# Moving a short convolution from TensorE to ScalarE and VectorE in a scheduled decoder layer

## The chip, the cores and the metric

The kernel runs on the 8 cores of one Trainium2 chip; every core works on one sequence of the batch. The time is that of the slowest core, in microseconds (us), as the device reports it. Below, PE is TensorE, DVE is VectorE, ACT is ScalarE, POOL is GpSimd and SP is SyncE, as the profile calls them. Some executions fall into a slow state, in which the cores of one die, sometimes of both, get a lower clock (0.95 to 0.81 of full speed, where the others have 0.99); only fast executions are compared.

The time before was 769.93 us (median of 6, 769.37 to 770.86).

## The reference

One decoder layer on x of 2048 x 1024 per core: two sub-layers, each with a norm before and a norm after, both scaled by a conditioning vector.

```python
def token_mixer(h, ...):
    z = einsum("bsd,dk->bsk", h, w_in)
    gb, gc, v, a, g = split(z)
    y_short = gb * causal_dwconv(gc * v, w_short, b_short)   # 3 taps, 512 channels
    u = causal_dwconv(a * sigmoid(g), w_cfm_dw, b_cfm_dw)    # 31 taps
    y_cfm = silu(layernorm(u))
    y = per_head_rmsnorm(concat(y_short, y_cfm)) * beta
    return einsum("bsm,md->bsd", y, w_out)                   # "out-projection"

h = modulate(rmsnorm(x, g_pre), shift1, scale1)
x = x + gate1 * rmsnorm(token_mixer(h), g_post)
h = modulate(rmsnorm(x, g_pre_ffn), shift2, scale2)
x = x + gate2 * rmsnorm(swiglu_ffn(h), g_post_ffn)
```

## The kernel before

The kernel is written as a list of operations with a cost each. When it is built, a scheduler of its own lays them out in time and fixes the order in which every engine works. The program gives each engine its list in that order, with waits on semaphores.

```python
def schedule(self):
    ...
    for s_, issue in succ[i]:        # when may a successor of o start, in the scheduler's reckoning?
        r = free[e] if issue or (e == "pe" and s_.eng == "pe") else \
            o.done + (0.0 if s_.eng != "pe" else MARGIN if o.dma is None else LATE ...)
    ...
MARGIN = 200.0                       # slack (ns) before an instruction of TensorE
```

The short convolution: a projection into one PSUM bank, three taps as matmuls with diagonal weights into a second one, then the product.

```python
def short(q):                                        # q: one of 4 chunks of 512 positions
    ... for j in range(4):
        proj(b3, wb, j * 1024, q, "pb", also=[b4])   # 8 matmuls 128x512
        act(bs, b3.v(), AF.Identity, bias=..., name="b_ev")
        for d in range(3):
            mm(b4.v(), dg3.v(i*128, i*128+128), rv_, d == 0, d == 2, name="sconv")
        dve("scalar_tensor_tensor", ..., name="ysh", in0=b4.v(), in1=bs, ...)
        ...                                          # squares, head statistics, norm
```

The out-projection, one tile of 128 positions after the other. Between its tiles TensorE works on other matmuls (the projections "pb" of later chunks, gate and up of the feed-forward part), here called filler.

```python
def outproj(q, pairs):
    for b in range(4):
        xt = Tile(xc_s).v()
        dma("pool", [(xt, xq[q, b])], ..., 1.35, "xload2")      # residual, on GpSimd's queue
        ...                                                     # and weight loads, same queue
        pt = pair('op', *pairs)                                 # two PSUM banks
        for n_, k in enumerate(korder):
            for hf in range(2):
                mm(pt.v(hf*512, hf*512+512, part=hf), yT..., wo..., name="oproj")
        post(pt.v(), xt, 0, 16 + i, xb_.v())
        dma("sp", [(x1q[q, b], xt)], [xt], ..., 1.95, "x1st")   # store; its landing frees xt
        last = norm_cast(xt, 32 + i, xb_.v())                   # pre-norm of the feed-forward part

def post(pv, xt, l, i, junk):
    tv = Tile(pg_s[l]).v()                                      # one product buffer
    dve("tensor_tensor", [pv, gtg], [tv], 1225, "po_g")         # product with the gate
    act(junk, pv, AF.Square, n=1024, accum=sm(SM_SSQ + i), name="po_sq")
    rsqrt_col(i, "po_rs", ...)          # two [128,1] steps on GpSimd: add EPS, then power -0.5
    dve("scalar_tensor_tensor", [tv, ("rs", i), xt], [xt], 1290, "po_add")
```

## Time and profile before

| | before |
|---|---|
| time, median | 769.93 us |
| spans of the cores in the profiled run | 764.2 to 768.6 us |
| TensorE busy | 736.7 us (96%) |
| out-projection, first to last matmul (core 4) | 208.6 to 335.6 us |

The head of the profile's page, for the slowest core: the span, then busy time and instructions of each engine.

```profile
span 768.6 us, 11317 instructions; the slowest of 8 cores (764.2 to 768.6 us)
...
PE 736.7 (96%) x4191; PEld 370.7 (48%) x4191; DVE 303.7 (40%) x464; ACT 266.7 (35%) x460; POOL 133.7 (17%) x271
```

The windows view of core 4: bounds and length of a stretch, then busy time (and instructions) of PE, PEld, DVE, ACT and POOL, the granted clock, the DMA share and GB/s.

```profile
0.00:33.00 33.00, 12.20 (x121) 7.39 (x122) 10.67 (x51) 9.00 (x18) 16.99 (x37) 0.95 0.94 190
...
211.00:338.00 127.00, 126.63 (x658) 59.62 (x657) 76.44 (x91) 74.19 (x118) 41.07 (x88) 1.00 0.74 178
```

In the out-projection stretch TensorE is busy all the time and the other three look half idle: VectorE 60%, ScalarE 58%, GpSimd 32%. The waits view of TensorE for the same stretch (waiter, what ended the wait, us in total, times, longest) has one entry:

```profile
PE ps L760 <- DVE xn_98 L594: 0.4, 1, 0.4
```

What a tile of the out-projection needs from the other engines is a chain. The timeline of one tile of core 4 (start, duration, engine, line, operation, what it writes and reads):

```profile
291.63 1.22 DVE L594 TENSOR_TENSOR pga_126<-ps,gtg_123 128x1024 f32<-128x1024 f32 x1 [1.78 <-PE ps L578]
...
292.94 1.02 ACT L590 ACTIVATE xn_96<-ps 128x1024 bf16<-128x1024 f32 x1 [1.85 <-DVE pga_126 L594]
...
294.22 0.22 POOL L598 TENSOR_SCALAR small<-small 128x1 f32<-128x1 f32 x1 [2.02 <-ACT xn_96 L590]
...
294.59 0.57 POOL L598 TENSOR_TENSOR small<-small 128x1 f32<-128x1 f32 x1
...
295.33 1.28 DVE L594 SCALAR_TENSOR_TENSOR xc_83<-pga_126,small,xc_83 128x1024 f32<-128x1024 f32 x1 [1.82 <-POOL small L598]
```

Product, squares, two small steps on GpSimd, add: from 291.63 to 296.62, that is 4.99 us, and the next tile's product may not start before, since there is one product buffer. In this part the first matmuls of successive tiles start at 287.8, 294.3, 300.8 and 307.3 us: one tile in 6.5 us.

### The profile page before, as it was taken

How to read it: one execution, taken by the hardware profiler on the slowest of the kernel's cores; microseconds unless marked ns; L12 is line 12 of the kernel's file. 1: busy time of each engine (PE TensorE's matmuls, PEld its weight loads, DVE VectorE, ACT ScalarE, POOL GpSimd, SP SyncE). 2: the span in 40 equal slices, each digit the busy share in tenths (PEclk: the TensorE clock that was granted, in tenths of full speed). 3: DMA queues.
4: the chain of work that ended last, by engine and by line, in shares of the span. 5: the costliest groups of instructions: out<-in, count | busy, mean ns of one | idle time of the engine just before them, and what ended most of it. 6: DMA issues, size and time to landing. Idle time of an engine off the chain costs nothing.

```text
span 768.6 us, 11317 instructions; the slowest of 8 cores (764.2 to 768.6 us)
## 1 busy us (share of the span) xinstructions
PE 736.7 (96%) x4191; PEld 370.7 (48%) x4191; DVE 303.7 (40%) x464; ACT 266.7 (35%) x460; POOL 133.7 (17%) x271
## 2 busy tenths in 40 slices
PE   0899999999999999999999999999999999999996
PEld 0587568544444444544444444444444444444442
DVE  3343876956657665553221221222221212112222
ACT  1255558884566854543111111111111111111112
POOL 4543212412103153332010000000000000000000
PEclk9998999999999999999999999999999999999999
DMA  8999538998694768889986395333434433001321
GB/s 185 197 240 218 99 86 115 145 164 138 157 194 139 182 153 204 202 211 195 179 156 119 55 142 133 109 110 110 110 55 82 84 56 54 1 0 56 113 87 75
DMA packets 36806, 98.16 MB, mean 128 GB/s; under 512 B 4112, under 2 KB 12432, under 8 KB 33424
## 3 DMA queue, kind: packets, MB, share of 16 engines
q0 software_dynamic: 20048, 66.92, 48.0%
q1 hardware_dynamic: 16704, 30.52, 12.1%
q8 instruction: 34, 0.56, 0.3%
q14 instruction: 20, 0.16, 0.1%
HBM read 125.54 MB, written 16.78 MB: 185 GB/s over the span
## 4 chain that ended last, share of the span: by engine, by line
PE 92%; DMA 2%; POOL 2%; ACT 1%; issue 1%; DVE 1%; DVEq 0%; SPq 0%; POOLq 0%; ACTq 0%
PE ps L578 90%; DMA xa_75<-x 2%; PE ps L760 2%; POOL small L598 1%; ACT hT L590 0%; DVE xc_85 L594 0%; ACT xn_97 L590 0%; ACT xn_98 L590 0%; DVE xn_98 L594 0%; POOL wdn_65 L610 0%; DVE xc_84 L594 0%; DVEq L419 0%; DVE pga_126 L594 0%; ACT xn_96 L590 0%; POOL wdn_64 L610 0%
## 5 line engine op out<-in xcount | busy, mean ns | idle before, releaser
L578 PE MATMUL ps<-hT,slot_46 128*128 128x512 bf16 x512 | 113.9, 379 | 0.0
L578 PE MATMUL ps<-wdn_64,actT 128*128 128x512 bf16 x512 | 113.3, 379 | 0.0
L578 PE MATMUL ps<-hT,slot_43 128*128 128x512 bf16 x448 | 102.1, 379 | 0.0
L578 PE MATMUL ps<-hT,slot_45 128*128 128x512 bf16 x448 | 99.6, 379 | 0.0
L578 PE MATMUL ps<-hT,slot_44 128*128 128x512 bf16 x384 | 84.7, 379 | 0.0
L578 PEld LDWEIGHTS ps<-wdn_64,actT 128*128 128x128 bf16 x512 | 50.1, 98 | 60.4
L578 PEld LDWEIGHTS ps<-hT,slot_46 128*128 128x128 bf16 x512 | 50.1, 98 | 58.2
L578 PEld LDWEIGHTS ps<-hT,slot_43 128*128 128x128 bf16 x448 | 43.5, 98 | 51.7 <-issue 1.4
L578 PEld LDWEIGHTS ps<-hT,slot_45 128*128 128x128 bf16 x448 | 43.7, 98 | 50.6
L598 POOL TENSOR_SCALAR small<-small 128x1 f32<-128x1 f32 x62 | 15.9, 256 | 291.9 <-ACT xn_95 L590 136.4
L578 PEld LDWEIGHTS ps<-hT,slot_44 128*128 128x128 bf16 x384 | 37.4, 98 | 45.2
L594 DVE TENSOR_TENSOR pgb_127<-ps,gtg_124 128x1024 f32<-128x1024 f32 (+1 forms) x17 | 19.7, 1162 | 76.0 <-PE ps L578 75.9
L578 PE MATMUL ps<-wdn_65,actT 128*128 128x512 bf16 x192 | 44.2, 379 | 0.0
L598 POOL TENSOR_TENSOR small<-small 128x1 f32<-128x1 f32 x62 | 38.7, 624 | 8.6 <-POOL small L598 0.6
L594 DVE TENSOR_TENSOR actT<-ev_107,ps 128x512 bf16<-128x512 f32 x22 | 15.1, 686 | 52.6 <-PE ps L578 52.6
L594 DVE TENSOR_TENSOR actT<-ev_108,ps 128x512 bf16<-128x512 f32 x22 | 15.1, 686 | 50.3 <-PE ps L578 50.1
L594 DVE TENSOR_TENSOR actT<-ev_110,ps 128x512 bf16<-128x512 f32 x22 | 15.1, 686 | 50.1 <-PE ps L578 50.1
L594 DVE TENSOR_TENSOR actT<-ev_109,ps 128x512 bf16<-128x512 f32 x22 | 15.1, 686 | 48.6 <-PE ps L578 48.6
L590 ACT ACTIVATE ev_107<-ps 128x512 f32<-128x512 f32 x22 | 13.1, 597 | 54.4 <-PE ps L578 54.4
L590 ACT ACTIVATE ev_110<-ps 128x512 f32<-128x512 f32 x22 | 13.1, 597 | 53.2 <-PE ps L578 53.2
L590 ACT ACTIVATE ev_108<-ps 128x512 f32<-128x512 f32 x22 | 13.1, 596 | 51.7 <-PE ps L578 51.7
L578 PE MATMUL ps<-wo_63,yT 128*128 128x512 bf16 x128 | 30.9, 379 | 0.0
(328 smaller groups left out, 963.8 us busy)
## 6 DMA issues: line engine op xcount, KB each, us to landing
slot_46<-wgu POOLq DMA_DIRECT2D x6, 1024.0 KB, 11.9
slot_44<-wgu POOLq DMA_DIRECT2D x6, 1024.0 KB, 10.6
slot_45<-wgu POOLq DMA_DIRECT2D x5, 1024.0 KB, 16.0
slot_43<-wgu POOLq DMA_DIRECT2D x5, 1024.0 KB, 11.2
wdn_64<-wdn POOLq DMA_DIRECT2D x16, 256.0 KB, 13.4
slot_44<-wada POOLq DMA_DIRECT2D x12, 256.0 KB, 10.7
slot_43<-wada POOLq DMA_DIRECT2D x2, 1024.0 KB, 12.7
slot_45<-wada POOLq DMA_DIRECT2D x8, 256.0 KB, 15.0
```

What stands on the lines that cost most here:

```text
L578: return P.op("pe", lambda e: e.matmul(out.ap, lhsT=lhsT.ap, rhs=rhs.ap, start=start, stop=stop), reads=[lhsT, rhs] + list(reads), writes= ...
L590: return P.op("act", lambda e: e.activation(out=out.ap, in_=in_.ap, **a), reads=[in_] + list(reads), writes=[out] + list(writes), cost=c, ...
L594: return P.op("dve", lambda e: getattr(e, meth)(**{k: val(v) for k, v in kw.items()}), reads=reads, writes=writes, cost=cost, lat=80.0, na ...
L598: return P.op("pool", lambda e: getattr(e, meth)(*a, **kw), reads=reads, writes=writes, cost=cost, lat=80.0, name=name)
L760: P.op("pe", lambda e, ov=ov, iv=iv: e.transpose(out=ov.ap, in_=iv.ap, identity=ident.t[:, :]), reads=[iv, ident.v()], writes=[ov], cost=6 ...
```

## The change

Its intent is to take 52 short-conv matmuls from TensorE, to halve the norm of the out-projection so that VectorE and ScalarE read its two PSUM banks at the same time, to build the weights of the long convolution more cheaply, to load inputs in another order, and to give the scheduler costs and slack that fit the chip better. The core of the diff:

```diff
 def short(q):
-    b3, b4 = bank('sm', 0, 1, 2, 3), bank('sm', 0, 1, 2, 3)
-    proj(b3, wb, j * 1024, q, "pb", also=[b4])
-    act(bs, b3.v(), AF.Identity, ..., name="b_ev")
-    for d in range(3): ...
-        mm(b4.v(), dg3.v(...), rv_, d == 0, d == 2, name="sconv")
+    ac = accd[q, j] if q < 2 else taps(q, j)      # chunks 0 and 1 were done early
+    b3 = bank('sm', 0, 1, 2, 3)
+    proj(b3, wb, j * 1024, q, "pb")
+def taps(q, j):
+    act(dst, src, AF.Identity, scale=w, bias=vc(V_BSH + j), npt=2, name="sconv")       # tap 0
+    dve("scalar_tensor_tensor", [src, dst, K_V], [dst], 210 + 1.055 * n * PT, "sconv") # taps 1, 2
 ...
 def post(pv, xt, l, i, junk):
+    if l == 0:
+        for z in range(2):
+            for y, hv_ in ((z, "g"), (1 - z, "s")):      # one bank for VectorE, the other for ScalarE
+                ... dve("tensor_tensor", ..., 690, "po_g") / act(..., AF.Square, ..., name="po_sq")
+        pool("tensor_scalar", ..., 350, "po_rs", ..., op0=ALU.add, op1=ALU.add)
+        pool("tensor_tensor", ..., 640, "po_rs", ..., op=ALU.pow)
+        dve("scalar_tensor_tensor", ..., 1290, "po_add")
 ...
-    for half in range(2): warm(...); xload(0, (2, 3), "pool") ...
+    NAMES = ["x00", "a0.x01.a1.x10.g0.g1.x11.g2.g3.h0.x2.wv.h1.x3"]    # order of the first loads
 ...
-    c = 200 + 0.833 * n + 70 * npt + (190 if accum is not None else 0)
+    c = 95 + 0.833 * n + (0, 60, 180)[npt] + (80 if accum is not None else 0)
 ...
-RAW_SHIFT = 250.0
-MARGIN = 200.0
+RAW_SHIFT = 400
+MARGIN = 500
+PAD = 40
```

## The prediction

> **What bounds the kernel now.** TensorE: 96% busy on the page, 92% of the chain of waits. Start-to-start times prove it: in the timeline sixteen 128x512 matmuls take from 82.29 to 85.75 us, 0.216 us each, which agrees with N/2.4+2.5 ns in the Trainium skill, "TensorE: Matmul & The Clock Gate" (Back-to-back issue gap). From 80 us to the end TensorE keeps that spacing; the waits list has only some 1 us for it after 92 us (0.5 us at 285 us and 0.45 us at 349 us, transposes waiting for xn_98 of the out-projection). Its other lost time is in the first 80 us: 17.4 us until the second x tile lands (17.8 us) and is normalised, 1.8 us at 28.5 us, 1.3 us at 73.5 us, and stretches at half clock (starts 0.427 us apart from 75 to 80 us; granted clock 0.76 between 66 and 80 us in the windows view). DMA is saturated until about 75 us.
>
> **Removed.** The short convolution's matmuls: 44 of 512 columns and 8 of 256. 44 x 0.216 + 8 x 0.109 = 10.4 us, all between 195 and 257 us where TensorE never waits, so all on the critical path. Also the diagonal weights (12 x 0.18 us VectorE) and 16 b_ev evictions (0.69 us ScalarE).
>
> **Added.** 16 accumulators: one ScalarE pass (est. 0.7 us, as b_ev of the same size) and two VectorE passes of 0.75 us (as glu and ysh). VectorE +24 us, ScalarE about even. Half lands in 143 to 200 us; both engines are full (19.6 and 19.5 of 20) only between 140 and 160 us, and VectorE is half free afterwards, so it is absorbed. The rest lands in 200 to 257 us, where VectorE is 63% busy. The convolution weights built from a broadcast (16 x 1.48 us) get perhaps 10 us of VectorE cheaper, off the path.
>
> **Moved.** The halved norm reads the two PSUM halves by VectorE and ScalarE at once. Per tile po_g (1.22) and po_sq (1.02+0.19) ran one after the other; now 2 x 0.69 beside 2 x (0.6+0.19): about 1 us less in a loop that has one product buffer and turned every 6 us. It keeps out-projection fed with fewer filler matmuls, and removes most of the two holes. The load order moves the same bytes and does not shorten the first wait. It should spread the sparse one-column matmuls that precede the half-clock stretch at 72 to 80 us; I credit 2.3 us, uncertain. Weight loads have 16 us of slack or more from 190 to 430 us, so arriving 10 us earlier does not run into DMA.
>
> **Sum.** 769.9 - 10.4 - 2.3 (start) - 0.9 (out-projection) = 756.3 us, range 752.5 to 760.5. Faster by over 2% 0.30, within 2% 0.69, slower 0.01.
>
> **What would show it.** TensorE matmuls down by 52; no cvb matmuls; span after 100 us shorter by about 11 us; TensorE waits after 92 us under 2 us; cw builds near 0.8 us; po_g as 32 halves near 0.69 us; the first gate-weight matmuls still near 35 us, and the half-clock stretch near 75 us shorter or gone.
>
> **What would make it wrong.** VectorE falling behind between 140 and 260 us (TensorE gaps before the y statistics, out-projection or its transposes); gate weights landing 5 us later and starting dense work later, costing 3 to 5 us; or a start that gains more, losing both the half-clock stretch and the waits before 35 us.

## The result and the profile after

The time after was 768.84 us (median of 20, slow ones included), beside 770.41 us for the kernel before on the same chip. The fast runs alone have medians of 766.76 (12 runs) and 770.24 us (35 runs). The ratio is 0.9956, with a 95% interval of 0.9945 to 0.9967: the same within 2%, about 3.4 us less. All ratios here are the mean time of one kernel's fast runs over that of the other's in the same rounds; the medians quoted can include slow runs, so a ratio isn't quite that of the medians.

The head of the page after:

```profile
span 765.9 us, 11358 instructions; the slowest of 8 cores (758.8 to 765.9 us)
...
PE 729.8 (95%) x4139; PEld 365.9 (48%) x4139; DVE 316.0 (41%) x505; ACT 270.6 (35%) x492; POOL 136.4 (18%) x271
```

The 52 matmuls are gone, yet TensorE's share of the span fell. The following table gives medians over the eight cores of start times in us. The waits of TensorE are the distance between the starts of successive matmuls beyond what their size takes at full clock, summed. They are idle time. Of the time lost at half clock they hold only what smaller matmuls lose: a 512-column matmul at half clock starts its successor 0.21 us late, which looks like a matmul that is missing from the record, and such excesses are left out. With half clock counted, the medians of most runs rise by 0.4 us at most, but those of e1, e3 and e4 (below) to 8.5, 6.9 and 8.6 us.

| milestone | before | after | difference |
|---|---|---|---|
| first gate-weight matmul | 33.3 | 34.6 | +1.3 |
| first matmul of the long convolution | 105.5 | 104.8 | -0.7 |
| first out-projection matmul | 211.3 | 213.1 | +1.8 |
| last out-projection matmul | 338.3 | 331.2 | -7.1 |
| last matmul | 760.3 | 755.2 | -5.1 |
| span | 767.1 | 761.6 | -5.5 |
| waits between first and last out-projection matmul | 0.7 | 6.0 | +5.2 |

So 5.2 of the 10.4 us came back as waits in one stretch. (Which fillers fall before the first out-projection matmul differs between the two orders, so single rows don't add up.) The windows view of core 4 after, same columns:

```profile
0.00:35.00 35.00, 12.54 (x123) 7.07 (x123) 10.95 (x45) 11.46 (x22) 20.68 (x44) 0.95 0.94 194
...
212.00:332.00 120.00, 115.71 (x599) 53.65 (x600) 83.77 (x115) 71.39 (x142) 48.30 (x88) 1.00 0.80 189
```

TensorE idles 4.3 us of these 120 where it idled 0.4 of 127. VectorE is at 70% and GpSimd at 40%: not full on average. The waits view of TensorE for this stretch:

```profile
PE ps L583 <- DVE pga_133 L599: 2.2, 2, 2.0
PE ps L583 <- ACT xn_104 L595: 1.2, 1, 1.2
PE ps L583 <- issue: 0.6, 2, 0.4
PE ps L762 <- DVE xn_105 L599: 0.5, 1, 0.5
```

The first two are projection or out-projection matmuls that wait for a PSUM bank which VectorE (pga, the product) or ScalarE (xn, the squares) has not read yet; the last are transposes that wait for a pre-norm (xn_105).

The average of VectorE hides the longest wait. The windows view of core 4 around it, and lines of the timeline:

```profile
231.00:237.00 6.00, 3.97 (x18) 1.45 (x17) 5.58 (x8) 5.18 (x10) 2.30 (x5) 1.00 0.54 203
...
234.03 0.74 DVE L599 SCALAR_TENSOR_TENSOR yT<-ys_120,vt,rs_124 128x512 bf16<-128x512 f32 x1
...
234.70 0.68 DVE L599 TENSOR_TENSOR pga_133<-ps,gtg_130 128x512 f32<-128x512 f32 x1
...
235.30 0.74 DVE L599 SCALAR_TENSOR_TENSOR yT<-ys_121,vt,rs_124 128x512 bf16<-128x512 f32 x1
...
235.96 0.68 DVE L599 TENSOR_TENSOR pga_133<-ps,gtg_130 128x512 f32<-128x512 f32 x1
...
236.89 2.10 PE L583 MATMUL ps<-hT,slot_43 128*128 128x512 bf16 x9 [2.00 <-DVE pga_133 L599]
```

VectorE is busy 5.58 of these 6 us (5.5 on the other cores), and its order puts two passes of the short convolution's norm (yT) before and between the two halves of the product. Here VectorE does fall behind.

The groups view of core 4 shows the pieces: new accumulator passes, the halved product, and the two GpSimd steps in the out-projection stretch (busy us, mean ns of one, idle time before them and what ended it). First the GpSimd lines of the kernel before, from 208 to 337 us:

```profile
L598 POOL TENSOR_TENSOR small<-small 128x1 f32<-128x1 f32 x30 | 17.1, 571 | 4.0
L598 POOL TENSOR_SCALAR small<-small 128x1 f32<-128x1 f32 x30 | 7.9, 265 | 73.2 <-ACT xn_95 L590 33.7 <-ACT xn_96 L590 18.3 <-ACT xn_97 L590 14.0
```

The same view of the kernel after, GpSimd from 212 to 332 us and the other two engines from 100 to 340 us:

```profile
L603 POOL TENSOR_TENSOR small<-small 128x1 f32<-128x1 f32 x30 | 18.3, 610 | 4.4 <-POOL small L603 0.4
L603 POOL TENSOR_SCALAR small<-small 128x1 f32<-128x1 f32 x30 | 13.3, 443 | 64.2 <-ACT xn_102 L595 33.5 <-ACT xn_103 L595 12.2 <-ACT xn_104 L595 10.9
...
L599 DVE TENSOR_TENSOR pga_133<-ps,gtg_130 128x512 f32<-128x512 f32 x32 | 22.0, 689 | 12.7 <-PE ps L583 8.2 <-ACT xn_102 L595 1.3 <-DVE pga_133 L599 0.9
...
L599 DVE SCALAR_TENSOR_TENSOR acc_58<-cvb_63,vt,acc_58 128x512 f32<-128x512 bf16 x5 | 3.7, 743 | 0.0
...
L595 ACT ACTIVATE acc_58<-cvb_63,vt 128x512 f32<-128x512 bf16 x3 | 2.4, 801 | 0.0
```

A GpSimd add on a 128x1 column takes 443 ns in the mean where it took 265. The timeline shows when it is long (core 4 after, parts of two neighbouring tiles):

```profile
263.00 0.22 POOL L603 TENSOR_SCALAR small<-small 128x1 f32<-128x1 f32 x1 [1.03 <-ACT xn_103 L595]
...
264.05 0.75 DVE L599 TENSOR_SCALAR xn_103<-xc_90,small 128x1024 bf16<-128x1024 f32 x1
264.05 0.83 POOL L603 TENSOR_SCALAR small<-small 128x1 f32<-128x1 f32 x1
265.03 0.56 POOL L603 TENSOR_TENSOR small<-small 128x1 f32<-128x1 f32 x1
...
265.84 1.28 DVE L599 SCALAR_TENSOR_TENSOR xc_91<-pga_133,small,xc_91 128x1024 f32<-128x1024 f32 x1 [1.03 <-POOL small L603]
```

The same add takes 0.22 us alone and 0.83 us beside VectorE's cast of the previous tile (264.05 to 264.80): it ends 0.08 us after the cast does. Over all cores, an add that starts under a VectorE pass whose operands are all in SBUF ends 0.08 us (or 0.16) after that pass, or after the next such pass where one follows at once (16 of 102), and a power step ends 0.42 us after it; beside VectorE passes that read PSUM they take 0.22 to 0.30 and 0.57 us. Between the first and the last out-projection matmul 24 of 232 adds took over 0.4 us before, and 88 of 232 after. Long adds alone don't make the waits, though: e1 (below) has only 32 of them and 7.8 us of waits, e10 has 48 of 168 and 1.4 us. The Trainium skill says this of the port that both engines share ("SBUF — State Buffer", Who interferes with whom): "only the shared port pair causes contention, and it's an exclusive lock". The trace agrees. Here the loser is on the critical chain: VectorE's add of the residual waits for GpSimd.

One more loss sits behind the longest wait. On cores 3 and 7 it is followed by a half-clock stretch. The windows view of core 7, the slowest after:

```profile
234.00:238.00 4.00, 3.97 (x19) 1.45 (x17) 3.31 (x5) 3.91 (x8) 1.68 (x3) 1.00 0.96 266
238.00:240.00 2.00, 0.24 (x2) 0.00 (x0) 2.00 (x5) 1.61 (x4) 0.66 (x2) 1.00 0.79 283
240.00:244.00 4.00, 3.76 (x10) 1.44 (x11) 3.43 (x5) 1.90 (x3) 2.58 (x5) 0.57 0.34 91
```

After the idle 2 us only 10 matmuls start in the 4 us from 240 to 244, where 19 started in the 4 us before, at a granted clock of 0.57: about 1.7 us more. That is one reason why the slowest core gained only 2.7 us in the profiled run and the median core 5.5. The other is larger: core 7 also started late (first matmul of the long convolution at 107.9 us, 104.8 on the median core). Core 3 has the same half-clock stretch but started early (103.0 us), and its span is 761.2 us.

### The profile page after: what moved, and what is told of

The parts are those of the page before. It is cut to its first block, busy times and chain, and to the rows that moved or that the text cites. A ratio compares the mean times of both kernels' runs of the same rounds, so it can differ in the third digit from the quotient of the medians.

```text
span 765.9 us, 11358 instructions; the slowest of 8 cores (758.8 to 765.9 us)
## 1 busy us (share of the span) xinstructions
PE 729.8 (95%) x4139; PEld 365.9 (48%) x4139; DVE 316.0 (41%) x505; ACT 270.6 (35%) x492; POOL 136.4 (18%) x271
## 4 chain that ended last, share of the span: by engine, by line
PE 88%; DMA 4%; POOL 2%; ACT 2%; issue 2%; DVE 2%; DVEq 0%; ACTq 0%; POOLq 0%
PE ps L583 86%; DMA wag_73<-wag 4%; POOL small L603 2%; PE ps L762 2%; ACT xn_103 L595 1%; DVE xc_90 L599 1%; ACT xn_104 L595 0%; ACT xn_105 L595 0%; DVE xc_91 L599 0%; ACT hT L595 0%; DVE pga_133 L599 0%; DVE xc_92 L599 0%; DVE xc_89 L599 0%; DVEq L419 0%; ACT xn_102 L595 0%
## 5 line engine op out<-in xcount | busy, mean ns | idle before, releaser
L583 PE MATMUL ps<-hT,slot_43 128*128 128x512 bf16 x448 | 102.2, 383 | 2.0 <-DVE pga_133 L599 2.0
L603 POOL TENSOR_SCALAR small<-small 128x1 f32<-128x1 f32 x62 | 20.2, 326 | 278.2 <-ACT xn_102 L595 140.8
L595 ACT ACTIVATE ev_117<-ps 128x512 f32<-128x512 f32 x22 | 13.1, 597 | 57.9 <-PE ps L583 57.9
L595 ACT ACTIVATE hT<-ps,small 128x512 bf16<-128x512 bf16 (+1 forms) x40 | 22.9, 636 | 26.0 <-PE ps L762 26.0
L595 ACT ACTIVATE ev_114<-ps 128x512 f32<-128x512 f32 x22 | 13.1, 596 | 53.4 <-PE ps L583 53.4
```

The lines of the kernel that those rows point to most:

```text
L583: return P.op("pe", lambda e: e.matmul(out.ap, lhsT=lhsT.ap, rhs=rhs.ap, start=start, stop=stop), reads=[lhsT, rhs] + list(reads), writes= ...
L595: return P.op("act", lambda e: e.activation(out=out.ap, in_=in_.ap, **a), reads=[in_] + list(reads), writes=[out] + list(writes), cost=c + ...
L603: return P.op("pool", lambda e: getattr(e, meth)(*a, **kw), reads=reads, writes=writes, cost=cost, lat=80.0, name=name)
```

## The experiments

Two theories stood first. A: the new VectorE passes of the short conv lengthen the chain of the out-projection's norm, through longer GpSimd steps (A1) or a full VectorE (A2). B: the new scheduler constants made an order with too little slack. After the first four runs a third took their place. P: TensorE's waits are a property of the fixed order. With fewer matmuls TensorE comes sooner to each tile, and any order that this scheduler makes from its durations leaves waits somewhere, because the chain's real durations aren't in it.

To put numbers on P, orders were laid out again with the durations and hand-over times that the traces show (for instance 0.18 us from TensorE to VectorE, 0.16 from ScalarE to GpSimd, 0.17 from GpSimd to VectorE, 0.25 from the squares to TensorE, and the rule above for GpSimd beside VectorE). These are estimates; they give 0.7 us of waits in the out-projection stretch for the kernel before (measured 0.7) and 3.8 for the changed one (measured 6.0).

| run | what it is | ratio to before | waits, estimated | waits, measured (median core) | median core in the profile |
|---|---|---|---|---|---|
| after | the change | 0.9956 | 3.8 | 6.0 | 761.6 |
| e1 | conv move alone, old constants | 0.9979 | - | 7.8 | 765.5 |
| e2 | the change without the conv move | 1.0103 | - | 5.1 | 771.0 |
| x1 | VectorE taps cut to 4 columns (wrong) | 0.9915 | - | 5.5 | 760.9 |
| x2 | VectorE doesn't wait for GpSimd (wrong) | 0.9899 | - | 2.8 | 758.1 |
| e3 | whole-tile norm | 0.9948 | 4.4 | 5.8 | 761.9 |
| e4 | old scheduler constants | 0.9960 | 4.1 | 8.0 | 764.3 |
| e5 | slack 350 | 0.9982 | 1.6 | 6.1 | 765.2 |
| e6 | slack 375 | 1.0004 | 4.8 | 9.5 | 766.2 |
| e7 | slack 350, store told as 4.0 us | 0.9953 | - | 4.7 (die 1) | slow |
| e8 | part of the inverse roots on ScalarE | 0.9962 | 1.1 | 2.2 | 760.8 |
| e9 | old order of loads | 0.9996 | 8.3 | 9.5 | 767.5 |
| e10 | e8 with the changed kernel's start | 0.9900 | 0.8 | 1.4 | 756.8 |

The kernel before had medians of 772.08, 772.27, 772.04 and 771.73 us in the four groups of rounds (e1, e2, x1, x2; e3 to e6; e7 to e9; e10).

### e1: the conv move alone

```diff
# from the kernel before: only taps(), its buffers and short(); norm, loads and constants (MARGIN = 200.0) as before
-proj(b3, wb, j * 1024, q, "pb", also=[b4])
-mm(b4.v(), dg3.v(...), rv_, d == 0, d == 2, name="sconv")
+ac = accd[q, j] if q < 2 else taps(q, j)
+proj(b3, wb, j * 1024, q, "pb")
```

> The kernel before with one part of the change alone: the short convolution on ScalarE and VectorE (52 matmuls fewer); old norm, old load order, old scheduler constants. Theory A (the convolution's VectorE passes fall into the out-projection's serial chain and turn the saved matmul time into TensorE waits): TensorE waits between the first and the last out-projection matmul rise from about 0.7 us to 5 us or more, and the time falls by only 3 to 6 us (764 to 767). Rival B (the new scheduler constants make the tight order; the convolution itself is harmless): no such waits under the old constants, and the time falls by 9 to 11 us (759 to 761).

It took 770.59 us, ratio 0.9979 (0.9965 to 0.9994). Waits of 7.1 to 8.2 us stand in the out-projection stretch on all cores, under the old constants and the old norm. B as the only cause falls. Of 10.4 us taken from TensorE, 7 came back. The time fell by 1.5 us, less than the 3 to 6 that A gave, so it doesn't confirm A in full either.

### e2: the change without the conv move

```diff
# from the changed kernel: short() and its matmuls as before
-ac = accd[q, j] if q < 2 else taps(q, j)
+mm(b4.v(), dg3.v(...), rv_, d == 0, d == 2, name="sconv")
```

> The changed kernel with the short convolution back on TensorE, all else as changed. Theory A: the waits in the out-projection stretch go back to about 1 us although 52 matmuls return; the time stays within 2 us of the changed kernel (766 to 769). Rival B: the waits of 6 us stay, the matmuls add 10 us, the time is 775 to 778.

It took 781.66 us, ratio 1.0103 (1.0072 to 1.0135): slower than the kernel before. With 4191 matmuls and no conv pass on VectorE it still waits 5.1 us, so the rest of the change makes waits of its own, in the order that it gets here, and A falls. The time is over B's 775 to 778 too. Its median core in the profile is 771.0 us, 9.4 more than the changed kernel's: moving the conv is worth nearly its 10.4 us when the rest of the change is in place (the order of work differs). Its slowest core was 9.9 us over the median one, with 10.7 us of waits.

### x1: nearly no tap work on VectorE

```diff
-dve("scalar_tensor_tensor", ..., "sconv", out=dst, in0=src, scalar=w, in1=dst, ...)
+dve("scalar_tensor_tensor", ..., "sconv", out=dst[:, :, 0:4], in0=src[:, :, 0:4], scalar=w, in1=dst[:, :, 0:4], ...)
```

> The changed kernel with the same order of instructions on every engine, but the convolution's VectorE passes cut to 4 columns per row (a wrong result on purpose). Theory A: TensorE waits in the out-projection stretch fall from 6.0 us to under 2 us and the time by 4 to 5 us (about 763). Rival B (the order itself is too tight, whatever the passes cost): the waits stay above 4.5 us, the time within 1.5 us of the changed kernel.

The order is the changed kernel's, the result is wrong (relative error 0.20). The waits fell from 6.0 to 5.5 us only. So the tap passes' time on VectorE, A2 and A1 through those passes, is not what TensorE waits for. (The longest wait stays at 1.8 us: none of VectorE's tap passes stands in the 6 us before its end, and VectorE is about as full there.) The ratio of 0.9915 is 3 us better than the changed kernel's all the same, while the median core of its profile is only 0.7 us shorter (1.5 us over all fast runs); where the rest came from stays open.

### x2: no wait for GpSimd

```diff
-dve("scalar_tensor_tensor", [tv, ("rs", i), xt], [xt], 1290, "po_add", ..., scalar=sm(SM_RS + i), in1=xt)
+dve("scalar_tensor_tensor", [tv, ("rs", i), xt], [xt], 1290, "po_add", ..., scalar=sm(SM_EXP), in1=xt)
# the cast of the pre-norm likewise; the waits of these VectorE operations on GpSimd are left out after scheduling
```

> The changed kernel with the same order, but in the out-projection stretch the VectorE steps that use the reciprocal root read a constant instead and no longer wait for GpSimd, whose steps still run (a wrong result on purpose). Theory A1 (the passes delay the chain mostly by making the GpSimd steps longer: its first step took 0.22 us beside an idle or PSUM-reading VectorE and 0.6 to 0.83 us beside a VectorE pass on SBUF operands): waits fall from 6.0 us to under 2 us, time 4 to 5 us less. Theory A2 (VectorE's queue is simply full): waits stay above 4 us, time within 2 us of the changed kernel.

Again the changed kernel's order, wrong (relative error 0.55). Waits of TensorE fell to 2.8 us on all cores but one (2.9), the time to 764.44 us. The waits view of core 4 in the same stretch:

```profile
PE ps L583 <- DVE pga L599: 1.2, 1, 1.2
PE ps L583 <- ACT xn L595: 0.6, 2, 0.5
PE ps L583 <- issue: 0.4, 1, 0.4
```

This lies between what A1 (under 2 us) and A2 (over 4 us) said. It splits the 6.0 us: 3.2 come through the wait for GpSimd, 2.8 are there without. The longest that remains stands at the same place as the changed kernel's longest, where VectorE is full.

### e3 to e6: other orders of nearly the same work

```diff
# e3: post() of layer 0 as before (whole tile)         # e4: old costs, MARGIN 200, RAW_SHIFT 250
# e5
-MARGIN = 500
+MARGIN = 350
# e6
-MARGIN = 500
+MARGIN = 375
```

> The changed kernel with one part undone: the out-projection norm of layer 0 is a whole-tile one again (one 128x1024 product, one 128x1024 square), everything else of the change stays. Theory H (the halved norm is to blame: its GpSimd step falls on the VectorE cast of the previous tile and takes 0.68 to 0.84 us in place of 0.22, and the halved passes are not shorter than the whole one): TensorE waits between first and last out-projection matmul fall from about 6 us (median core of the changed kernel, 0.74 before) to under 3 us, and the time falls 2 us or more under the changed kernel, ratio to before 0.993 or less. Theory P (the waits are made by the fixed order, and any order made by this scheduler for the lighter TensorE has them; laid out with the durations of the traces, an estimate, this order has about 0.6 us more of them than the changed kernel's): waits 5 to 8 us, ratio to before 0.994 to 0.999.

> The changed kernel with the scheduler's constants of before (costs, slack 200 ns, shift 250); the work, the halved norm and the order of the loads stay as changed. Theory B (the new constants make a tight order): waits of TensorE in the out-projection stretch under 3 us, ratio to before 0.991 or less. Theory P (any order has such waits once the conv matmuls are gone; laid out with the durations of the traces, an estimate, this order has 4 us, like the changed kernel's 3.8): 4.5 to 7 us of waits, ratio to before 0.993 to 0.999.

> The changed kernel with one number changed: the slack that the scheduler adds before a TensorE instruction is 350 ns in place of 500. The work of every engine is the same, only the fixed order differs. Theory P (the waits are the order's; laid out with the durations of the traces, an estimate, this order has 1.6 us of waits in the out-projection stretch where the changed kernel's has 3.8, and its last matmul comes 4.4 us earlier): waits 2 to 4 us instead of 6, the time 3 to 5 us under the changed kernel, ratio to before 0.988 to 0.992. Theory W (the waits belong to the work: the norm's chain of VectorE, ScalarE and GpSimd steps per tile is full): waits 5 us or more, the time within 1 us of the changed kernel's, ratio 0.994 to 0.997.

> As e5 with 375 ns in place of 350: 25 ns more slack. Theory P: the order is another one again, and a bad one (estimate: 4.8 us of waits in the out-projection stretch, the last matmul 0.9 us later than the changed kernel's and 5.3 us later than e5's): waits 5.5 to 8 us, ratio to before 0.995 to 0.999, clearly slower than e5. Theory W: like e5 within 1 us.

e3 measured 5.8 us of waits and 0.9948 (0.9917 to 0.9979): an order without the halved norm has as many waits, with 49 long adds of 232 in place of 88, so H falls. e4 measured 8.0 us, more than P's 4.5 to 7, and 0.9960 (0.9938 to 0.9981, of only two fast runs): B falls again. e6 went the way that P said, but further: 9.5 us of waits where 5.5 to 8 were expected, and 1.0004 where 0.995 to 0.999 were. e5 was a miss: 1.6 us estimated, 2 to 4 expected, 6.1 measured, and it differed by core, from 4.5 to 8.1, where the changed kernel has the same waits on all. The waits of e5 and e6 differ by 3.4 us in the median; the intervals of their ratios (0.9965 to 0.9999 and 0.9975 to 1.0032) overlap, so that the times alone wouldn't tell them apart.

What the estimate lacked shows in e5's timeline of GpSimd on core 1:

```profile
280.95 1.09 POOL L615 DMA_DIRECT2D wdn<-wdn  x2
287.45 0.53 POOL L615 DMA_DIRECT2D xc<-x  x1 [5.40 <-DMA x1s<-xc]
287.96 1.08 POOL L615 DMA_DIRECT2D wdn<-wdn  x2
289.14 0.30 POOL L603 TENSOR_SCALAR small<-small 128x1 f32<-128x1 f32 x1
```

The squares for that add were ready at 286.2 us. But a load of x stood before it in GpSimd's queue and waited 5.4 us for a store to land and free its buffer, and two weight loads came after it, 0.54 us each. The add ran 3 us late, and TensorE then waited 2.3 us and lost more at half clock. Stores took 5.9 us in the median from issue to landing in this stretch of the changed kernel, but single ones from 2.6 to 12.6 us (the 5.2 to 6.4 us of the next expectation are medians by buffer); the scheduler reckoned one figure for all, 4.65.

### e7: tell the scheduler how long a store takes

```diff
# from e5
-dma("sp", [(x1q[q, b], xt)], [xt], [("x1d", i)], 1.95, "x1st")
+dma("sp", [(x1q[q, b], xt)], [xt], [("x1d", i)], 4.0, "x1st")
```

> e5 (slack 350) with one more number changed: the scheduler is told that a store of the residual takes 4.0 us in place of 1.95 (the traces show 5.2 to 6.4 us from issue to landing, the scheduler reckons 4.65 in all, 6.7 with this). No engine's work changes. Theory Q (GpSimd works its queue in order; loads of x for the next chunk wait in it for a store to land, up to 5.4 us on core 1 of e5, and the norm's two small steps stand behind them, which made the 2.28 and 2.10 us waits of TensorE in e5): with the loads placed later the waits of TensorE between first and last out-projection matmul fall from 6.1 us (median core of e5) to 2 to 3.5 us, and are alike on all cores; time 3 us under e5 and about 2 us or more under the changed kernel, ratio to before 0.989 to 0.993. Theory W (the chain of work per tile is full whatever the order): waits stay above 5 us.

Only two runs were fast, and the profile fell in the slow state, on die 0. On die 1, which was not disturbed, the waits are 4.7, 4.7, 4.7 and 5.2 us: alike on its cores, as Q expects, and less than e5's 6.1, but not the 2 to 3.5 expected. The ratio is 0.9953 (0.9931 to 0.9974). The standing in GpSimd's queue is part of e5's miss, and something else adds some 2 us that no run here isolates. The ratio is over the 0.989 to 0.993 expected.

### e8: meant to beat both

```diff
# from the changed kernel; first of 4 chunks, and its pre-norms likewise (EPS, 1e-6, isn't added in the four out-projection norms)
+if i < 20:
+    act(rv, sm(SM_SSQ + i), AF.Ln, n=1, bias=sm(SM_SS2), npt=1, name="po_rs")
+    act(rv, rv, AF.Exp, n=1, scale=-0.5, name="po_rs")
+else: ...                                        # the two GpSimd steps
-("x1d", i)], 1.95, "x1st")
+("x1d", i)], 4.0, "x1st")
-SHUF, MARGIN, P.shift = 0.5, 500, 100
+SHUF, MARGIN, P.shift = 0.0, 200, 75             # GpSimd steps told as 222 and 800 ns
```

> Meant to beat both. The changed kernel, with the inverse square root of chunk 0's four out-projection tiles (and their pre-norms) as logarithm and exponential on ScalarE in place of the two GpSimd steps (the table of the short conv's norm is loaded then), the store told to the scheduler as 4.0 us, GpSimd steps told as 222 and 800 ns, slack 200 ns, the conv passes' shift 75 and no shuffle shift. Theories P and Q (waits come from the order and from standing behind others in GpSimd's queue; laid out with the durations of the traces, an estimate, 1.1 us of waits, the last matmul 4.3 us before the changed kernel's): waits 1.5 to 3 us, time 3 to 5 us under the changed kernel, ratio to before 0.987 to 0.992. Theory W: waits stay above 4.5 us.

The waits fell to 2.2 us (1.5 to 2.3 on six cores, 4.0 and 5.2 on cores 0 and 7, which each also lost about 1.7 us in 3.4 us at half clock near 326 us), as P and Q said and against W. The time did not follow: 769.29 us, 0.9962 (0.9941 to 0.9983). The first gate-weight matmul came at 37.9 us instead of 34.6 and the first conv matmul at 107.1 instead of 104.8: what the out-projection gained, the start lost.

### e9: the old order of loads

```diff
-NAMES = ["x00", "a0.x01.a1.x10.g0.g1.x11.g2.g3.h0.x2.wv.h1.x3"]
+xload(0, (0, 1), "sp") ... wag = [wload(wag_d[0], 2048, "wag0", wag_s)] ...   # as before
```

> The changed kernel with the order of the loads and the program order of the start as before. For the start: the prediction gave the new order a gain of 2.3 us; the profiled runs show the first gate-weight matmul 1.3 us later and the first conv matmul 0.7 us earlier with it. If the new order helps, the first conv matmul comes 1 us or more later here (over 105.8 us on the median core, 104.8 in the changed kernel); if not, at 104 to 105. For the rest, theory P (laid out with the durations of the traces, an estimate, this order has 8.3 us of waits in the out-projection stretch): 7 to 10 us of waits, ratio to before 0.998 to 1.005. Theory W: 5 to 6.5 us of waits as in the changed kernel, ratio 0.994 to 0.998.

The first conv matmul came at 106.0 us in the median, 1.2 after the changed kernel's, over cores that reach from 104.9 to 109.4. So the new order of the loads is worth about 1 us, and the spread between cores is larger than that. Waits: 9.5 us, ratio 0.9996 (0.9972 to 1.0019), near the 8.3 that the estimate said and far from W's 5 to 6.5.

### e10: e8 with the changed kernel's start

```diff
# from e8: first GpSimd step told as 350 ns, P.shift = 50, and
-o.done + (... MARGIN if o.dma is None ...)
+o.done + (... (500.0 if o.start < 1.3e5 else MARGIN) if o.dma is None ...)
```

> Meant to beat both. As e8 (inverse square roots of chunk 0 on ScalarE, store told as 4.0 us, shuffle 0, slack 200 ns), but the slack stays 500 ns for what runs before 130 us, so that the start keeps the changed kernel's order, GpSimd's first step told as 350 ns and the conv passes' shift 50. Laid out with the durations of the traces (an estimate): 0.8 us of waits in the out-projection stretch (e8's estimate was 1.1, measured 2.1; the changed kernel's 3.8, measured 5.9). Theory P: waits 1.5 to 2.5 us on cores without a half-clock stretch, the first gate-weight matmul back at 33 to 36 us (37.9 in e8), median core 756 to 759 us, ratio to before 0.987 to 0.993, a few us under the changed kernel. If the gain is lost elsewhere again (start, half-clock stretches), waits are short as said but the ratio is 0.994 to 0.997, as for e8.

It took 762.88 us (762.11 to 766.69) beside 771.73, ratio 0.9900 (0.9879 to 0.9920), with a correct result: the fastest correct kernel, better than both. From the head of its page:

```profile
PE 729.6 (96%) x4139; PEld 366.3 (48%) x4139; DVE 316.0 (42%) x505; ACT 273.0 (36%) x508; POOL 126.9 (17%) x255
```

The windows view of core 4 in the out-projection stretch:

```profile
210.00:326.00 116.00, 114.72 (x591) 53.88 (x602) 83.41 (x115) 73.09 (x155) 35.21 (x70) 1.00 0.82 195
```

And its waits view of TensorE there, the only line:

```profile
PE ps L583 <- issue: 0.5, 3, 0.2
```

All conv passes are still on VectorE (83.4 us busy here, 83.8 in the changed kernel) and the norm is still halved. VectorE is even full for 12 us in this order, and TensorE doesn't wait there (windows view of core 4):

```profile
228.00:240.00 12.00, 11.95 (x56) 5.41 (x56) 12.00 (x18) 11.01 (x23) 1.59 (x3) 1.00 0.86 241
```

TensorE's waits are 1.2 to 1.6 us on every core. The median core of the profile is 756.8 us, 10.3 less than before (about 10 over all fast runs): nearly the whole of the 10.4 us. The time of the slowest core gained a little less, 8.9 us between the medians, since its start and half-clock stretches vary from core to core (first conv matmul from 102.2 to 109.9 us). What the order and what the four tiles' steps on ScalarE did for this isn't separated: no run has e10's constants with all steps on GpSimd.

## Why the prediction was wrong, point by point

- **"TensorE bound ... 0.216 us each."** Right. The trace keeps the spacing that the Trainium skill states ("TensorE: Matmul & The Clock Gate", Back-to-back issue gap, N/2.4 + 2.5 ns). That section calls it the gap of an isolated matmul and gives about 131 ns at 512 columns for a stream of weight loads and matmuls; this stream, with as many weight loads as matmuls, keeps 216 ns. And e10 shows that what is taken from TensorE comes off the span one for one when nothing else makes it wait.
- **"Removed ... 10.4 us, all on the critical path."** Right as a sum (52 matmuls fewer; 9.4 us between the median cores of e2 and the changed kernel, 10.3 in e10), but it isn't a gain by itself. The kernel before was an order in which, where tiles follow each other closely, 3.0 us of filler beside 3.5 us of out-projection covered a chain of 5 us; with less for TensorE to do, another order has to cover it again.
- **"VectorE is half free afterwards, so it is absorbed."** Right as to the work: the passes measured 743 ns (0.75 predicted) on VectorE and 801 ns on ScalarE (0.7 estimated), and x1 shows that leaving them out hardly changes the waits. But VectorE wasn't half free everywhere: it was busy 5.58 of the 6 us before the longest wait's end.
- **"About 1 us less in a loop ... keeps out-projection fed with fewer filler matmuls, and removes most of the two holes."** This is the step that failed, the overlap: TensorE was to stay fed with less filler. It stood at -0.9 us in the sum, and waits of +5.2 us came in its place. From the first product to the end of the add a tile of core 4 took 5.3 us before and 5.2 us after (medians of the 13 and 14 tiles with no transposes between): what the halves save, the GpSimd add, which the prediction counted as short, takes back where it meets VectorE's cast (0.83 us in place of 0.22). And the new order gave each tile less filler: the later tiles start every 5.7 us (288.9, 294.7, 300.4) in place of 6.5, so that this chain, which had 1.5 us to spare, makes TensorE wait 0.1 to 0.35 us at several of them. Most of the 6.0 us are two waits in earlier tiles: 2.2 us at 234.5, where VectorE is full, and 1.3 us at 262.1, where the chain of the tile before came late (its add took 0.85 us and its power step 0.85, both beside VectorE passes). An order without the halving has about as many waits (e3, 5.8 against 6.0 us).
- **"TensorE waits after 92 us under 2 us."** Wrong: over 6 us. The prediction named the danger: VectorE "falling behind between 140 and 260 us", with gaps before out-projection. That happened for one wait of 2.2 us, although VectorE was 70% busy on average, but not through the passes that the change added (x1), and a VectorE that is full for 12 us needn't make TensorE wait (e10). It gave the danger no term in the sum.
- **"I credit 2.3 us" for the start.** Mis-sized: the first conv matmul came 0.7 us earlier in the median of the profiled runs, and e9 gives the order of the loads about 1.2 us. The half-clock time that it was to shorten didn't change: from 35 to 103 us TensorE ran at half clock for 3.6 us before and 3.7 us after in the median, and from 1.4 to 7.7 us by core after. "Gate weights landing 5 us later" was partly so: x was loaded before them, and the first gate-weight matmul came 1.3 us later.
- **The sum.** On the median core: -10.4 (matmuls) + 5.2 (waits in the out-projection stretch) - 0.7 (start to the first conv matmul) leaves +0.4 for the rest of the measured -5.5. The slowest core, which is the time, gained 2.7 us in the profiled run and about 3.4 by the ratio: a late start and the half-clock stretch behind the longest wait took the difference on core 7.
- **What stays open.** Why e7's waits and the changed kernel's are some 2 us above what was expected or estimated, where x1 gained beyond its waits, and how much of e10's gain is the order and how much the steps moved to ScalarE.

So this much of the cause is shown: what was removed came back as waits of TensorE in the out-projection stretch; the waits need no particular piece of the change (e1, e2, e3, e4, x1); they are halved without the wait for GpSimd (x2); 25 ns of slack in the scheduler move them by 3 us with the same work (e5 and e6); and another order of the conv move and the halved norm, with four tiles' small steps taken from GpSimd, has nearly none (e10). That every order of this scheduler leaves such waits, as P had it, isn't so, by e10; that the order alone, without the steps on ScalarE, can remove them isn't shown.

## What to carry to other kernels

When an engine that was always busy gets less work, ask what the others have to deliver per tile, and how much of that was covered by the work that goes away; a share of 60 to 70% busy over a stretch says nothing about a serial chain of small steps, nor about 6 us within it in which the engine is full. In a kernel with a fixed order, an estimate of a change is one of an order: lay the new order out with durations from the trace, contention and waiting DMA issues in the queue included, before crediting the work removed. Look twice at tiny steps of a critical chain on an engine that shares a port with its neighbour and issues DMAs in the same queue: the wait for them was 3.2 of the 6.0 us here (x2).

## What the Trainium skill lacked or had wrong

- "SBUF — State Buffer" (Who interferes with whom) says the loser of the shared port "fully blocks" for the whole instruction. The trace agrees but for a step's first 0.15 us or so: an add that takes 0.22 us alone ends 0.08 us after VectorE's cast, and a power step that takes 0.57 us alone ends 0.42 us after VectorE's pass, so 0.14 and 0.15 us of them ran before or beside the lock. The section has no number for steps as small as 128x1.
- The same section says that whoever issues first gets the port for the whole instruction. For the adds the traces agree: of 513 that started 5 ns or more before a VectorE pass on SBUF, with no other such pass running, 506 were not held up (all runs). For the power step they don't: of 65 that started 0.1 to 0.4 us before a VectorE cast 62 still ended 0.04 us after it, up to 1.13 us long in place of 0.57 (at 42.80 us on core 0 before: 1.05 us, the cast from 43.07 to 43.81), while of 113 that started up to 0.4 us before a two-input VectorE pass none was held up. Start times of GpSimd are rough in the trace.
- "TensorE: Matmul & The Clock Gate" (Why this matters for your kernels) advises no idle gaps over about 3 us between bursts of matmuls. Here shorter ones cost clock too: of 63 waits of 2.0 to 3.0 us between 120 and 700 us (all cores of all runs with a fast profile), 34 were followed by a half-clock stretch (three or more of the next 12 matmuls), as on core 7 after (granted clock 0.57 from 240 to 244 us); of waits from 0.25 to 2.0 us, 17 of 621.
- I found no page that warns, with a number, of DMA issues that stand before compute steps in GpSimd's queue: one waited 5.4 us for its buffer in e5 and the norm's step behind it with it, and each issue in that view took 0.53 to 0.55 us of GpSimd even when it waited for nothing.
